# Padding tiles so that all operands of TensorE begin at one byte modulo 512, in a tuned encoder-layer kernel

## The chip, the cores and the metric

The kernel runs on one core of a Trainium2 chip, in one launch. The metric is the device time in microseconds (us), the median of several runs. A profile is one execution recorded by the hardware profiler. TensorE (PE) multiplies matrices; its loading of the stationary operand is listed apart, as PEld. VectorE (DVE), ScalarE (ACT) and GpSimd (POOL) do the element-wise work; SyncE (SP) issues most DMAs. On-chip memory has 128 partitions; a tile takes the same byte range in each of them, and "place" below means the first byte of that range.

## The reference

One layer on 1024 tokens of width 1024, in float32, with three sub-layers, each with an RMSNorm before and after and a residual sum:

```
h = rms_norm(x);  q, k, v, u, gates = split(h @ w_in)
o_attn = stick_breaking_attention(q, k, v)      # 8 heads x 64, strictly causal
o_ssm  = s5_branch(u)                           # complex-diagonal scan, gelu, sigmoid GLU
merged = gate_attn * (o_attn @ w_branch_attn) + gate_ssm * (o_ssm @ w_branch_ssm)
x = x + rms_norm(merged @ w_out)
x = x + rms_norm(cross_attention(rms_norm(x), mem))        # 4 heads, 256 memory tokens
x = x + rms_norm(conv_ffn(rms_norm(x)))         # up to 2 x 2816, causal conv 3, gelu gate, down
```

Stick-breaking attention weighs key s for query t by sigmoid(z_ts) times the product of (1 - sigmoid(z_tj)) over the keys j between them.

## The kernel before, in words

Every product is made in split precision: an operand is kept as a high part (rounded to the matmul's input format) and a low part (the rest), and `mm3` (L140 to L143) issues three matmuls for each 128-deep step: high x high, high x low, low x high. Nearly all of these are 128x128 weights against 512 moving columns. For each of them TensorE loads 128 columns of the stationary operand while the matmul before still runs.

The stages, in order of time:

- value and u projection (`tokens`, L423): hT, the normalised input (high and low, in pool ha), is stationary, in u with every eighth column; the weights move. The fourth chunk of these weights lies in two tiles of its own, wx (pool px).
- the S5 branch (`intra`, `flip_w`, `states`, `outputs`), its small matmuls and transposes set among jobs of the gate projection (`Job.step`, L265; hT moves), then the GLU (`glu_job`, L925): tiles yh, yl of pool pg move.
- stick-breaking attention (L996 to L1084): scores z from q, k, kl (pool pqk), sigmoids s1 and s2 (pool pat), a reversed scan on DVE, transposes of s1 with ident, then weighing (wth, wtl against vv). A list of groups with due times, made in advance, sets these among projection jobs: three 512-wide matmuls of a job, then one group.
- memory keys and values (`mem_k`, L1256, 256 wide; `mem_v`, L1270): the memory's tiles lie in pqk, reused as r_q and r_k; the merge of the branches (`merge`, L1316), whose moving operands lie in pqk (r_q, r_k, r_kl) and pc (oh, ol).
- output projection (`mix_out`, L1378), transposes of the new rows (xr in pool p5), queries, cross-attention (`xa_score` L1647, `xa_weigh` L1669, tiles pt, ph, pl in pool p6a) with projection steps between, its output projection, and the rows' norms (xr in pool p6).
- the gated MLP (`product`, L1905, then `mm_step`, L2186), by a seven-product scheme, from pools wpool, ha and hb; one early operand, S4a, lies in pool p6b.

In the first four stages and the output projection the order of instructions on TensorE, ScalarE, VectorE and GpSimd follows from due times (`at`, L227; `pe`, L797); later TensorE's order is the program's. SP takes DMAs in program order.

Pools are stacked: left pools from the bottom, right pools from the top of the memory. Within a pool, tiles lie in the order in which they are first asked for, rounded up to 32 bytes, the buffers of one tag side by side. When a pool is closed, the next one takes its place, and a tile's first write waits for the old tiles that it covers.

For attention's s1 rows there are four tags, one for each pair c of query blocks, each with two buffers that are (2c + 2) x 128 columns wide; block j = 0 of the pair uses (2c + 1) x 128 of them and j = 1 all.

By the declared sizes the tiles that TensorE reads begin at these bytes modulo 512:

| tiles | before | after |
|---|---|---|
| weights (wpool), hT and all of ha, all of hb | 288 | 288 |
| ident | 128 | 288 |
| wx (px); Tt, Ug, rc, y8 (pb) | 448 | 288 |
| U; W, F1, E1 (pt); yh, yl (pg) | 160 | 288 |
| Y1 | 480 | 288 |
| q, k, kl and r_q, r_k, r_kl (pqk); s1, vv, wth, wtl (pat); oh, ol (pc) | 480 | 288 |
| xr of p5 | 64 | 288 |
| pt; ph, pl (p6a) | 352; 416 | 288 |
| S4a (p6b) | 416 | 288 |
| xr of p6 | 32 | 32 |

Of the kernel before, what the change touches and what calls it, by code (L numbers as in the profile page):

```python
# [11 lines left out]
F32 = mybir.dt.float32  # L12
# [8 lines left out]
P = 128  # L21
# [24 lines left out]
def kernel(ctx: ExitStack, tc: tile.TileContext, a: dict, out: bass.AP, dbg=None):  # L46
# [4 lines left out]
    const = ctx.enter_context(tc.tile_pool(name="const", bufs=1, side="left"))  # L51
# [14 lines left out]
    td = [dpool.tile([4, P, 512], F32, name=f"td{q}") for q in range(NF // 2)]  # L66


    ident = const.tile([P, P], F32, name="ident")
    make_identity(nc, ident)  # L70
    zcol = const.tile([P, 1], F32, name="zcol")
    G.memset(zcol, 0.0)
    mhalf = const.tile([P, 1], F32, name="mhalf")
    G.memset(mhalf, -0.5)
    bgate = const.tile([P, 16], F32, name="bgate")
    bglu = const.tile([P, 4], F32, name="bglu")
    wr = ExitStack()
    pr_ = wr.enter_context(tc.tile_pool(name="pr", bufs=1, side="left"))
    gcol = pr_.tile([P, 2, KT], F32, name="gcol")
    rates_x = pr_.tile([P, 2, KT], F32, name="rates_x")  # L80
    rates_m = pr_.tile([P, 2], F32, name="rates_m")
    row_k = pr_.tile([P, 512], F32, name="row_k")
    rx_d = dpool.tile([KT, P], F32, name="rx_d")
    rm_d = dpool.tile([2, P], F32, name="rm_d")

# [38 lines left out]
    def f(ap):  # L124
        return ap.bitcast(F32)
# [87 lines left out]
    def gain_row(pool, name):  # L213
        g = pool.tile([P, D], F32, tag=name, name=name, bufs=1)
        dma(g, a[name].partition_broadcast(P))
        return g
# [10 lines left out]
    def at(t, go):  # L227
        heapq.heappush(events, (t, len(seen), go))
        seen.append(t)
# [48 lines left out]
    def rates_load(h):  # L278
        dma(row_k, rx_d[4 * h:4 * h + 4].rearrange("t p -> (t p)").partition_broadcast(P))
# [15 lines left out]
    def qk_job(pp, key):  # L295
        def out(t, h, sl, acc):
            Q, K, kl = qk[pp]
            hi, scale = (K, 1.0) if key else (Q, 0.125)

            lanes = [(slice(64 * i, 64 * i + 64), slice(64 - 64 * i, 128 - 64 * i)) for i in range(2)]  # L300

            def scaled(t):
                V.tensor_tensor(acc, acc, row_k, op=ALU.mult)
                rates_load(1 - h)

            def high(t):
                for i, (ln, xl) in enumerate(lanes):
                    C.mul(hi[i][ln, sl], acc[ln], scale)
                    if key:
                        dma(f(hi[i][xl, sl]), f(hi[i][ln, sl]))  # L310

            def low(t):
                for i, (ln, xl) in enumerate(lanes):
                    lo = kl[i][ln, sl] if key else hi[i][xl, sl]
                    V.scalar_tensor_tensor(lo, acc[ln], scale, f(hi[i][ln, sl]), op0=ALU.mult, op1=ALU.subtract)
                    if key:
                        dma(f(kl[i][xl, sl]), f(lo))

            if key:
                at(t, scaled)  # L320
            at(t + (0.8 if key else 0.0), high)
            at(t + (2.2 if key else 1.4), low)

        def start():

            qk[pp] = [[pqk.tile([P, S], F32R, tag=f"{n}{i}", name=f"{n}{i}") for i in range(2)] for n in ("q", "k", "kl")]

        return Job(a["w_in_T"][4 + pp if key else pp], out, start if key else None)

# [19 lines left out]
    pa = ra.enter_context(tc.tile_pool(name="pa", bufs=1, side="right"))  # L349
# [6 lines left out]
    U = pa.tile([P, 32, 8, 16], F32, name="U")  # L356
    sp = pq.tile([P, 3, 32], F32, name="sp")
    sbc = pq.tile([P, 4, 512], F32, name="sbc")
    dm = pa.tile([P, 32, 16], F32, name="dm")
    xt, rows_x, raw, pair = {}, {}, {}, {}  # L360
    sums_x = p0.tile([P, KT], F32, name="sums_x")

# [159 lines left out]
    turns = pa.tile([P, 7, 32], F32, name="turns")  # L522
    pr = pa.tile([P, 32, 9], F32, name="pr")
    pi = pa.tile([P, 32, 9], F32, name="pi")
    gc = [P, 32, 16]
    X, Xs, Y1, Y2 = (pa.tile(gc, F32, name=n) for n in ("X", "Xs", "Y1", "Y2"))

    def constants():
        G.memset(ec, math.e)
# [341 lines left out]
    while timed:  # L871
        t0, _, took, go, n = heapq.heappop(timed)
# [52 lines left out]
    def glu_job(m):  # L925
        def out(t, h, sl, acc):
            def put(t):
                if h == 0:
                    og[m] = open_g.pool.tile([P, S], F32, tag="og", name="og", bufs=2)
                C.activation(og[m][:, sl], acc, AF.Sigmoid, bias=bglu[:, m:m + 1])  # L930

            def gated(t):
                V.tensor_tensor(og[m][:, sl], og[m][:, sl], yT[m][:, sl], op=ALU.mult)
                if h:
                    dma(os_d[m], og[m])

            at(t, put)
            at(t + 0.8, gated)

        return Job(a["w_glu_T"][m], out, n=512, steps=4, operand=lambda k, sl: (yh[k][:, sl], yl[k][:, sl]))  # L940

    clock = max(clock, g0_ + 5.2)
    for m in range(4):
        j = glu_job(m)
# [18 lines left out]
    pqk = rqk.enter_context(tc.tile_pool(name="pqk", bufs=2, side="right", reuse_waits="tile"))  # L963
    rat = ExitStack()
    pat = rat.enter_context(tc.tile_pool(name="pat", bufs=2, side="right", reuse_waits="tile"))
# [28 lines left out]
    rows_of = {}  # L994

    def scores(t, n, c, j, n0, n1):  # L996

        (pp, hd), qi = divmod(n, 2), 2 * c + j
        Q, K, kl = qk[pp]
        nk = (qi + 1) * P  # L1000
        diag = n1 == nk
        qs = slice(qi * P, (qi + 1) * P)
        z = ps("z")[:, :n1 - n0]
        T.matmul(z, Q[hd][:, qs], K[hd][:, n0:n1], start=True, stop=False, skip_group_check=True)
        T.matmul(z, Q[hd][:, qs], kl[hd][:, n0:n1], start=False, stop=True, skip_group_check=True)  # L1005
        w = (n1 - n0) / 512.0

        def sig(t):
            if diag:
                rows_of[n, c, j] = (pat.tile([P, (2 * c + 2) * P], F32, tag=f"s1{c}", name="s1", bufs=2),  # L1010
                                    pat.tile([P, S], F32, tag="s2", name="s2", bufs=3))
            s1, s2 = rows_of[n, c, j]
            e = n1 - 1 if diag else n1
            if diag:
                G.memset(s1[:, e:n1], 0.0)
            C.activation(s2[:, n0:n1], z, AF.Sigmoid, scale=rates_x[:, 1, qi:qi + 1])  # L1016
            C.activation(s1[:, n0:e], z[:, :e - n0], AF.Sigmoid, scale=rates_x[:, 0, qi:qi + 1])

        def scan(t):
            s2 = rows_of[n, c, j][1]  # L1020
            add = begin[:, 512 - (n1 - n0):][:, ::-1] if diag else zcol.to_broadcast([P, n1 - n0])
            V.tensor_tensor_scan(s2[:, n0:n1][:, ::-1], s2[:, n0:n1][:, ::-1], add,  # L1022
                                 0.0 if diag else s2[:, n1:n1 + 1], op0=ALU.mult, op1=ALU.add)

        def rest(t):
            s1, s2 = rows_of[n, c, j]
            e = n1 - 1 if diag else n1
            G.tensor_tensor(s1[:, n0:e], s1[:, n0:e], s2[:, n0 + 1:e + 1], op=ALU.mult)  # L1028

        t += 0.5 * w + 0.4  # L1030
        at(t, sig)
        at(t + 0.7 * w + 0.2, scan)
        at(t + 2.2 * w + 0.5, rest)
# [76 lines left out]
    t, nf, begun, last_z = 0.0, 0, {}, 1e9  # L1110
# [110 lines left out]
    pool_of, row_of = {}, {}  # L1221
# [180 lines left out]

    def x1_load(t):
        x5[t] = pool_of["5"].tile([P, D], F32, tag="xr", name="xr", bufs=3)
        dma(x5[t], a["x"][t * P:(t + 1) * P, :])

    def x1_rates(h):
# [146 lines left out]
    p6 = r6.enter_context(tc.tile_pool(name="p6", bufs=1, side="right", reuse_waits="tile"))  # L1554
    gap = gain_row(p6, "g_xa_post")
    gfp = gain_row(p6, "g_ffn_pre")
    r6a = ExitStack()
    p6a = r6a.enter_context(tc.tile_pool(name="p6a", bufs=1, side="right", reuse_waits="tile"))

    have, yu, su, lows, again = {}, {}, {}, {}, [0]  # L1560

    def wo_chunk(x):
# [84 lines left out]
    def xa_score(h, hd, tp, fill):  # L1647

        qt = q2[h, hd // 2]
        sc = ps("a").rearrange("p (t m) -> p t m", t=2)  # L1650
        for t in range(2):
            ts_ = slice((2 * tp + t) * P, (2 * tp + t + 1) * P)
            for k in range(2):
                m = 2 * (hd % 2) + k
                mm3(sc[:, t], qt[:, 0, m, ts_], qt[:, 1, m, ts_], mk[:, 0, 2 * hd + k, :], mk[:, 1, 2 * hd + k, :],
                    k == 0, k == 1)
        fill(2)
        mx = p6a.tile([P, 2], F32, tag="mx", name="mx", bufs=2)
        V.reduce_max(mx, sc, axis=AX.X)
        V.tensor_scalar(mx, mx, -1.0 / 16, None, op0=ALU.mult)  # L1660
        pt = p6a.tile(s3, F32, tag="pt", name="pt", bufs=3)
        sm = p6a.tile([P, 2], F32, tag="sm", name="sm", bufs=2)
        for t in range(2):
            C.activation(pt[:, t], sc[:, t], AF.Exp, bias=mx[:, t:t + 1], scale=1.0 / 16, accum_out=sm[:, t:t + 1])
        V.reciprocal(sm, sm)
        V.tensor_tensor(pt, pt, bc(sm, 2, s3), op=ALU.mult)
        return pt
# [676 lines left out]
```

## Time and profile before

| | |
|---|---|
| median of 3 runs | 1656.94 us (1653.69 to 1658.94) |
| span of the profiled execution | 1653.9 us |
| instructions | 22415 |
| matmuls | 8062 |
| DVE, ACT, POOL busy | 1163.6, 880.1, 202.2 us |
| DMA | 279.26 MB, mean 169 GB/s |

How to read the lines below. A group's line has the source line, engine, operation, tiles as out<-in, shape and count; then busy time, mean ns of one and idle time of the engine before it, with what ended it. Matmuls are pipelined: the next starts before the one before it has ended, and the ends are modelled, so a duration of 0.39 us doesn't mean that matmuls start 0.39 us apart. The spacing of their starts is seen in the timeline (first column: start in us) or from a window's length and count. In a matmul's line one of the names after the arrow is the stationary and one the moving operand.

### The profile page before, as it was taken

Reading aid. Unit: us, or ns where it says so; the run is one execution under the profiler, and the core shown is the slowest. Engines: PE = TensorE matmul, PEld = TensorE weight load, DVE = VectorE, ACT = ScalarE, POOL = GpSimd, SP = SyncE. Lnnn points to the kernel's source line nnn. Section 1 sums busy time; section 2 is a strip of 40 time slices with the busy share of each in tenths; the row PEclk is TensorE's granted clock in tenths of the full one; section 3 lists DMA queues with packets and bytes.
Section 4 is the critical chain, followed back from the end, with each engine's and each line's share of the span. In section 5 each row is a group of like instructions: output and inputs, shape, how many; then the busy total and the mean of one; then the engine's idle time right before and its main releaser. Section 6 shows DMA issues by size and latency. Waiting matters only on the chain.

```text
span 1653.9 us, 22415 instructions
## 1 busy us (share of the span) xinstructions
PE 1633.8 (99%) x8062; PEld 1379.8 (83%) x8062; DVE 1163.6 (70%) x1616; ACT 880.1 (53%) x1459; POOL 202.2 (12%) x296
## 2 busy tenths in 40 slices
PE   9999999999999999999999999999999999999998
PEld 7998887888888988888888888888888888888886
DVE  6778637776866687467655678888887788775473
ACT  5434346676766544344444556656565556654441
POOL 5000002333332000011000000111111111000010
PEclk9999999999999999999999999999999999999999
DMA  9412144232433954464423574677777676688672
GB/s 323 124 46 66 61 144 110 71 102 80 113 99 127 336 190 136 158 211 158 141 69 129 205 271 175 187 210 211 214 195 206 186 203 185 210 311 280 192 237 81
DMA packets 125439, 279.26 MB, mean 169 GB/s; under 512 B 23696, under 2 KB 28304, under 8 KB 125200
## 3 DMA queue, kind: packets, MB, share of 16 engines
q1 hardware_dynamic: 113664, 251.35, 46.1%
q0 software_dynamic: 9360, 18.09, 6.3%
q10 hardware_dynamic: 2304, 8.39, 1.3%
q8 instruction: 63, 1.03, 0.3%
q14 instruction: 48, 0.39, 0.1%
HBM read 203.98 MB, written 67.38 MB: 164 GB/s over the span
## 4 chain that ended last, share of the span: by engine, by line
PE 89%; DVE 6%; DMA 2%; ACT 2%; issue 1%; POOL 0%; SPq 0%; DVEq 0%; POOLq 0%; ACTq 0%
PE ps_p L1921 8%; PE ps_p L1919 8%; PE ps_p L1920 8%; PE ps_f L141 7%; PE ps_f L143 7%; PE ps_f L142 6%; PE ps_d L2190 4%; PE ps_d L2189 4%; PE ps_d L2191 4%; PE ps_m L141 3%; PE ps_m L143 3%; PE ps_m L142 3%; PE ps_o L1067 2%; PE ps_w L1042 2%; PE ps_z L141 1%; PE ps_z L142 1%
## 5 line engine op out<-in xcount | busy, mean ns | idle before, releaser
L141 PE MATMUL ps_f<-hT,wh 128*128 128x512 f32 x384 | 161.3, 420 | 0.0
L143 PE MATMUL ps_f<-hT,wl 128*128 128x512 f32 x384 | 150.8, 393 | 0.0
L142 PE MATMUL ps_f<-hT,wh 128*128 128x512 f32 x384 | 150.6, 392 | 0.0
L1920 PE MATMUL ps_p<-qS,bm 128*128 128x512 f32 (+2 forms) x368 | 140.4, 382 | 1.7 <-DVE qS L1744 1.7
L1919 PE MATMUL ps_p<-qS,bm 128*128 128x512 f32 (+2 forms) x368 | 140.5, 382 | 1.4 <-DVE uu L1937 0.9
L1921 PE MATMUL ps_p<-qS,bm 128*128 128x512 f32 (+2 forms) x368 | 140.5, 382 | 0.0
L147 DVE TENSOR_TENSOR dn<-raw,dn 128x1024 fp32r<-128x1024 f32 x77 | 93.4, 1223 | 63.0 <-ACT dn L146 59.2
L146 ACT CAST dn<-raw 128x1024 fp32r<-128x1024 f32 x77 | 80.5, 1054 | 87.2 <-PE ps_d L2191 36.4
L2189 PE MATMUL ps_d<-dn 128*128 128x512 f32 x308 | 119.8, 389 | 0.0
L2190 PE MATMUL ps_d<-dn 128*128 128x512 f32 x308 | 119.8, 389 | 0.0
L2191 PE MATMUL ps_d<-dn 128*128 128x512 f32 x308 | 119.8, 389 | 0.0
L1028 POOL TENSOR_TENSOR s<-s,s 128x127 f32<-128x127 f32 (+4 forms) x96 | 89.9, 937 | 223.8 <-DVE s L1022 178.6
L1921 PE MATMUL ps_p<-qA,bm 128*128 128x512 f32 (+2 forms) x272 | 105.1, 386 | 0.5 <-DVE bm L1850 0.5
L1919 PE MATMUL ps_p<-qA,bm 128*128 128x512 f32 (+2 forms) x272 | 105.3, 387 | 0.0
L1920 PE MATMUL ps_p<-qA,bm 128*128 128x512 f32 (+2 forms) x272 | 105.0, 386 | 0.0
L1932 ACT COPY uu<-ps_p 128x512 f32<-128x512 f32 (+2 forms) x90 | 51.5, 572 | 90.0 <-PE ps_p L1921 90.0
L1862 POOL DMA_DIRECT2D bm<-in_ffn_up_T x61 | 52.7, 864 | 356.6 <-ACT bm L1861 144.2
L143 PEld LDWEIGHTS ps_f<-hT,wl 128*128 128x128 f32 x384 | 72.1, 188 | 16.3
L1016 ACT ACTIVATE s<-ps_z,rates_x 128x128 f32<-128x128 f32 (+3 forms) x96 | 56.3, 587 | 54.0 <-PE ps_z L1005 47.8
L1919 PEld LDWEIGHTS ps_p<-qS,bm 128*128 128x128 f32 x368 | 69.2, 188 | 15.2 <-ACT uu L1932 2.2
L1920 PEld LDWEIGHTS ps_p<-qS,bm 128*128 128x128 f32 x368 | 69.2, 188 | 15.1 <-DVE qS L1744 2.0
L1921 PEld LDWEIGHTS ps_p<-qS,bm 128*128 128x128 f32 x368 | 69.3, 188 | 13.2
(544 smaller groups left out, 4462.2 us busy)
## 6 DMA issues: line engine op xcount, KB each, us to landing
raw<-sd SPq DMA_DIRECT2D x77, 256.0 KB, 3.5
bm<-in_ffn_up_T POOLq DMA_DIRECT2D x61, 256.0 KB, 5.4
ws<-in_w_in_T SPq DMA_DIRECT2D x24, 512.0 KB, 3.3
ws<-in_xa_wo_N SPq DMA_DIRECT2D x23, 512.0 KB, 4.3
wv<-in_ffn_up_T SPq DMA_DIRECT2D x22, 512.0 KB, 4.0
wg<-in_ffn_up_T SPq DMA_DIRECT2D x22, 512.0 KB, 3.8
dr<-in_ffn_down SPq DMA_DIRECT2D x22, 512.0 KB, 6.4
td<-st SPq DMA_DIRECT2D x44, 256.0 KB, 5.9
```

The costliest lines, as they stand in the source:

```text
L141: T.matmul(acc, sh, mh, start=first, stop=False)
L142: T.matmul(acc, sh, ml, start=False, stop=False)
L143: T.matmul(acc, sl, mh, start=False, stop=last)
L146: C.copy(dh, src)
L147: (lo or V).tensor_tensor(dl, src, f(dh), op=ALU.subtract)
L1028: G.tensor_tensor(s1[:, n0:e], s1[:, n0:e], s2[:, n0 + 1:e + 1], op=ALU.mult)
L1919: T.matmul(acc, bm[:, 0, ks], q[:, 0, k, cs], start=alone and k == 0, stop=False, skip_group_check=True)
L1920: T.matmul(acc, bm[:, 0, ks], q[:, 1, k, cs], start=False, stop=False, skip_group_check=True)
L1921: T.matmul(acc, bm[:, 1, ks], q[:, 0, k, cs], start=False, stop=k == 3, skip_group_check=True)
L2189: T.matmul(acc[i], v[:, 0, 0, sl], v[:, 0, 1], start=first, stop=False, skip_group_check=True)
L2190: T.matmul(acc[i], v[:, 0, 0, sl], v[:, 1, 1], start=False, stop=False, skip_group_check=True)
L2191: T.matmul(acc[i], v[:, 1, 0, sl], v[:, 0, 1], start=False, stop=last, skip_group_check=True)
```

## The change

The tiles are moved; no instruction is added, removed or put elsewhere in its queue. In the constants' pool four small tiles (160 bytes in all) are asked for ahead of ident. In pool pr the row tile comes first, and a pad of 88 floats makes the small tiles after it come to 512 bytes. Pads of 48 floats in pqk, 96 in pa, 72 in p5, 32 in p6 and 96 in p6a shift what lies below them. In pa, five 2 KB tiles come right after U. In p6a, sm is asked for before pt. The s1 rows get one buffer for each block j, as wide as its row, in place of two of the wider width; that takes 2 KB less. A pad tile is never written or read.

```diff
+    zcol = const.tile([P, 1], F32, name="zcol")
+    mhalf = const.tile([P, 1], F32, name="mhalf")
+    bgate = const.tile([P, 16], F32, name="bgate")
+    bglu = const.tile([P, 4], F32, name="bglu")
     ident = const.tile([P, P], F32, name="ident")
     make_identity(nc, ident)
...
+    row_k = pr_.tile([P, 512], F32, name="row_k")
     gcol = pr_.tile([P, 2, KT], F32, name="gcol")
     rates_x = pr_.tile([P, 2, KT], F32, name="rates_x")
     rates_m = pr_.tile([P, 2], F32, name="rates_m")
-    row_k = pr_.tile([P, 512], F32, name="row_k")
+    pr_.tile([P, 88], F32, name="pad_r")
...
             qk[pp] = [[pqk.tile([P, S], F32R, tag=f"{n}{i}", name=f"{n}{i}") for i in range(2)] for n in ("q", "k", "kl")]
+            if pp == 0:
+                pqk.tile([P, 48], F32, name="pad_qk", bufs=1)
...
-    dm = pa.tile([P, 32, 16], F32, name="dm")
+    gc = [P, 32, 16]
+    X, Xs, Y1, Y2, dm = (pa.tile(gc, F32, name=n) for n in ("X", "Xs", "Y1", "Y2", "dm"))
...
-    gc = [P, 32, 16]
-    X, Xs, Y1, Y2 = (pa.tile(gc, F32, name=n) for n in ("X", "Xs", "Y1", "Y2"))
+    pa.tile([P, 96], F32, name="pad_a")
...
-                rows_of[n, c, j] = (pat.tile([P, (2 * c + 2) * P], F32, tag=f"s1{c}", name="s1", bufs=2),
+                rows_of[n, c, j] = (pat.tile([P, (2 * c + j + 1) * P], F32, tag=f"s1{c}{j}", name="s1", bufs=1),
                                     pat.tile([P, S], F32, tag="s2", name="s2", bufs=3))
...
         x5[t] = pool_of["5"].tile([P, D], F32, tag="xr", name="xr", bufs=3)
+        if t == 0:
+            pool_of["5"].tile([P, 72], F32, name="pad_5")
...
     gfp = gain_row(p6, "g_ffn_pre")
+    p6.tile([P, 32], F32, name="pad_6")
...
     p6a = r6a.enter_context(tc.tile_pool(name="p6a", bufs=1, side="right", reuse_waits="tile"))
+    p6a.tile([P, 96], F32, name="pad_6a")
...
         mx = p6a.tile([P, 2], F32, tag="mx", name="mx", bufs=2)
+        sm = p6a.tile([P, 2], F32, tag="sm", name="sm", bufs=2)
...
         pt = p6a.tile(s3, F32, tag="pt", name="pt", bufs=3)
-        sm = p6a.tile([P, 2], F32, tag="sm", name="sm", bufs=2)
```

More of the change, by code (lines that the diff above doesn't have):

```diff
@@ L66 @@
     td = [dpool.tile([4, P, 512], F32, name=f"td{q}") for q in range(NF // 2)]
+    zcol = const.tile([P, 1], F32, name="zcol")
+    mhalf = const.tile([P, 1], F32, name="mhalf")
+    bgate = const.tile([P, 16], F32, name="bgate")
+    bglu = const.tile([P, 4], F32, name="bglu")
     ident = const.tile([P, P], F32, name="ident")
     make_identity(nc, ident)
-    zcol = const.tile([P, 1], F32, name="zcol")
     G.memset(zcol, 0.0)
-    mhalf = const.tile([P, 1], F32, name="mhalf")
     G.memset(mhalf, -0.5)
-    bgate = const.tile([P, 16], F32, name="bgate")
-    bglu = const.tile([P, 4], F32, name="bglu")
     wr = ExitStack()
     pr_ = wr.enter_context(tc.tile_pool(name="pr", bufs=1, side="left"))
+    row_k = pr_.tile([P, 512], F32, name="row_k")
     gcol = pr_.tile([P, 2, KT], F32, name="gcol")
```

## The prediction

> **What bounds the kernel now.** I read the page first (busy time, slices, chain), then windows of single stages, then groups by form, then the timeline of TensorE where it changes from one kind of work to another.
>
> ```profile
> span 1653.9 us, 22415 instructions
> PE 1633.8 (99%) x8062; PEld 1379.8 (83%) x8062; DVE 1163.6 (70%) x1616; ACT 880.1 (53%) x1459; POOL 202.2 (12%) x296
> PE   9999999999999999999999999999999999999998
> PEclk9999999999999999999999999999999999999999
> PE 89%; DVE 6%; DMA 2%; ACT 2%; issue 1%; POOL 0%; SPq 0%; DVEq 0%; POOLq 0%; ACTq 0%
> ```
>
> TensorE is the bound from end to end: 99% busy, nine tenths or more in all slices but the last, at the full granted clock, and 89% of the chain. Nothing else can shorten the kernel by much; only a shorter time from one matmul's start to the next one's can. The change leaves the number and the order of the instructions as they are and moves tiles, so the question is whether a tile's place sets that time. The windows say by how much equal matmuls differ.
>
> ```profile
> core 0: us, PE busy (x) PEld busy (x) DVE busy (x) ACT busy (x) POOL busy (x), PEclk, DMA share, GB/s
> 218.50:240.50 22.00, 22.00 (x96) 17.72 (x95) 7.97 (x11) 9.18 (x13) 0.00 (x0) 1.00 0.44 157
> 260.00:535.00 275.00, 273.29 (x1525) 232.56 (x1524) 201.81 (x269) 193.15 (x403) 91.74 (x157) 1.00 0.34 97
> 583.00:671.00 88.00, 88.00 (x379) 70.91 (x378) 68.94 (x100) 41.33 (x59) 0.00 (x0) 1.00 0.46 147
> 1440.00:1640.00 200.00, 200.00 (x884) 165.64 (x884) 120.99 (x119) 92.17 (x108) 6.73 (x6) 1.00 0.67 227
> ```
>
> Columns: length, then busy time and count of each engine, granted clock, DMA. Three of these windows (GLU, branch merge, down projection) hold nothing but 128x512 matmuls without a gap. A matmul that only touches an edge is counted too, so the spacing is the length plus one duration (0.39 us) over the count: 88.39/379 = 233.2 ns in the merge, 22.39/96 = 233.2 ns in the GLU, 200.39/884 = 226.7 ns in the down projection. Clock, shape and number of weight loads are the same; DVE, ACT and DMA are busier in the fast window than in the GLU, so they aren't the cause. What differs is the place: in the down projection both operands begin at 288 modulo 512, in the merge the moving one at 480 and the weights at 288, in the GLU 160 and 288.
>
> The modelled duration in the groups by form carries the same 6 to 7 ns, which allows small groups to be compared:
>
> ```profile
> L2190 PE MATMUL ps_d<-dn 128*128 128x512 f32 x308 | 119.8, 389 | 0.0
> L141 PE MATMUL ps_z<-wh,mh 128*128 128x512 f32 x32 | 12.5, 390 | 0.0
> L142 PE MATMUL ps_w<-ol,wh 128*128 128x512 f32 x32 | 12.7, 396 | 0.0
> L142 PE MATMUL ps_f<-yl,wh 128*128 128x512 f32 x32 | 12.6, 395 | 0.0
> L142 PE MATMUL ps_z<-wl,r_q 128*128 128x512 f32 x8 | 3.2, 398 | 0.0
> L141 PE MATMUL ps_o<-wh,r_q 128*128 128x512 f32 x8 | 3.2, 396 | 0.0
> L142 PE MATMUL ps_m<-wx,hT 128*128 128x512 f32 x32 | 12.9, 402 | 0.0
> ```
>
> The first two rows have both operands at 288, the other five do not. The output projection right after the merge (ps_z<-wh,mh) is at 390, though it goes round the same four banks in the same way. So I take the place to be the cause there.
>
> **The change part by part.** Moving each tile to 288:
>
> (a) Branch merge, L1316: 8 x 2 x 2 x 4 x 3 = 384 matmuls in an unbroken run, 384 x (233.2 - 226.7) = -2.5 us. (b) GLU, L925: 4 x 2 x 4 x 3 = 96, 96 x 6.5 = -0.6 us. (c) Memory values, L1270: 96 matmuls at 397 (mean of the two r_q rows) against 389.5: -0.7 us. (d) wx in the value projection: 48 of the 96 wx matmuls have contiguous weights; their row mixes them with the u projection, so it gives bounds, from 0 to 48 x (402 - 389) = 0.6 us; I take half, -0.3 us, since the strided half can't become aligned. All four lie on the path, with hardly any idle time of TensorE in between: -4.1 us.
>
> [...]
>
> (e) Narrower matmuls. Here an aligned pair is not the faster one:
>
> ```profile
> L142 PE MATMUL ps_w<-r_k,wh 128*128 128x256 f32 x16 | 4.5, 281 | 0.0
> L143 PE MATMUL ps_a<-mk,q 128*128 128x256 f32 x64 | 18.1, 283 | 0.0
> L142 PE MATMUL ps_f<-hT,wh 128*128 128x512 f32 x384 | 150.6, 392 | 0.0
> L143 PE MATMUL ps_f<-hT,wl 128*128 128x512 f32 x384 | 150.8, 393 | 0.0
> L1004 PE MATMUL ps_z<-k,q 128*128 128x512 f32 x48 | 19.2, 400 | 0.0
> L1005 PE MATMUL ps_z<-kl,q 128*128 128x512 f32 x48 | 18.8, 393 | 0.0
> L142 PE MATMUL ps_m<-h2l,wh 128*128 128x512 f32 x88 | 34.4, 391 | 0.0
> ```
>
> The memory keys (r_k at 480, weights at 288) take 281, the cross-attention scores (both at 288) 283. Aligned, the 192 matmuls of L1256 should become like the scores: 192 x 2 = +0.4 us.
>
> (f) Mixed stages: SSM, stick-breaking attention (window 260 to 535, 1525 matmuls), cross-attention. hT and wh there are at 288 already, and still at 392 and 393, since every third matmul is followed by scores, transposes or weighting. Would aligning those others help? The timeline shows a stretch in which everything has been at 288 all along:
>
> ```profile
> start us, us, engine line op out<-in xcount [idle before <-releaser]
> 798.35 0.28 PE L142 MATMUL ps_a<-mk,q 128*128 128x256 f32 x1
> 798.47 0.28 PE L143 MATMUL ps_a<-mk,q 128*128 128x256 f32 x1
> 798.59 0.40 PE L141 MATMUL ps_m<-h2h,wh 128*128 128x512 f32 x1
> 798.82 0.40 PE L142 MATMUL ps_m<-h2l,wh 128*128 128x512 f32 x1
> 799.06 0.39 PE L143 MATMUL ps_m<-h2h,wl 128*128 128x512 f32 x1
> 799.29 0.40 PE L141 MATMUL ps_m<-h2h,wh 128*128 128x512 f32 x1
> 799.52 0.39 PE L142 MATMUL ps_m<-h2l,wh 128*128 128x512 f32 x1
> 799.75 0.39 PE L143 MATMUL ps_m<-h2h,wl 128*128 128x512 f32 x1
> 799.98 0.39 PE L141 MATMUL ps_m<-h2h,wh 128*128 128x512 f32 x1
> 800.20 0.39 PE L142 MATMUL ps_m<-h2l,wh 128*128 128x512 f32 x1
> ```
>
> After a row of 256-wide matmuls the first six 512-wide ones take 799.98 - 798.59 = 1.39 us, 232 ns each; only then do they settle. A change of width upsets the rhythm by itself, aligned or not, and it comes back after about six matmuls. Attention changes its work after three, so it never gets there. I take 0 for the mixed stages. Bounds: if all of their 512-wide matmuls fell to 389, 3 x 384 x 3.5 = 4.0 us (L141 taken like its two neighbours), 48 x (11 + 4) = 0.7 us for the z scores and 3 x 88 x 2.5 = 0.7 us for the queries, together -5.4 us. If they all took the 0.40 us of the passage above, the same 1,152 + 96 + 264 = 1,512 matmuls would cost 7 ns more each, +10.6 us. I stand near zero, since the passage (232 ns) and attention's rows (392 and 393, 3 to 4 above 389) agree.
>
> (g) Strided weights of the u projection (every eighth column of hT) and Tt's slices start at other bytes whatever the pool does: 0. FFN up and down: already at 288, and their pools don't move: 0.
>
> (h) Buffers and waits. The sigmoid rows: two buffers, used in turn by j = 0 and 1, become one of each j; each is rewritten one head later as before, so nobody waits longer. 4 x 512 bytes come free, which pay for the pads. No instruction is added (the pads are never written) and none changes its place in a queue. What can move is which old tile a new one lies on, and so what its first write waits for. The pools are shifted by 512 bytes or less (tiles inside attention's pool by up to 2 KB), so most tiles cover the same old ones. The one place that I found next to the path is g_xa_post's buffer in p6, which lay over 96 bytes of g_xa_pre's and now clears it:
>
> ```profile
> 789.50 1.28 DVE L1428 SCALAR_TENSOR_TENSOR xr<-y,rstd,g_xa_pre 128x1024 f32<-128x1024 f32 x1 [0.72 <-POOL rstd L210]
> 791.95 0.33 SPq L131 DMA_DIRECT2D ws<-in_xa_wq_T  x1
> 792.34 0.42 SPq L215 DMA_DIRECT2D g_xa_post<-in_g_xa_post  x1
> ```
>
> g_xa_pre was last read until 790.8, but on SP's queue the load stands behind a load of wq that goes at 791.95 anyway: 0. Had a shift gone the other way, that queue would hold up wq's later loads; I see none that does.
>
> Sum: -4.1 + 0.4 = -3.7 us. The profiled execution had a span of 1653.9 us and would come to 1650.2; that span is 3.0 us below the median of the runs, 1656.94, so a run comes to 1656.94 - 3.7 = 1653.2 us. A measurement of this kernel can tell about 0.3%, 5.0 us, from no change; the forecast is within it.
>
> **The rivals.** *All stages settle.* If it is the misaligned transposes, probabilities and values that upset the rhythm, attention settles too: -5.4 us on top, the +0.4 falls away: -4.1 - 5.4 = -9.5, 1647.4 us. For it: every break in attention today includes a tile at 480 or 128. Against it: the passage at 798, which is all aligned and upset. Chance 0.20.
>
> *The place is not the cause.* The slow runs share more than the byte: they read from the upper, right-hand pools. [...] Then nothing moves, 1656.9 us. Against it: the output projection takes moving weights and settles at once, and pools at 480, at 160 and at 448 are all slow. Chance 0.17.
>
> *Aligned reads collide (slower).* If a common start makes the weight load and the moving read meet at every line, long unbroken runs settle around it but broken ones pay each time. The 1,512 matmuls of (f) then take 0.40 us: +10.6 + 0.4 - 4.1 = +6.9, 1663.8 us. It undoes the gain from 3.7/1,512 = 2.4 ns per matmul on. For it: 281 against 283 in (e). Against it: the agreement in (f). Chance 0.06.
>
> **How the numbers follow.** My forecast has the rest, 0.57. Of it about 0.11 lies beyond 5.0 us of gain, where half of (f)'s lower bound comes true or the runs scatter (1653.69 to 1658.94 before); so faster by over 0.3%: 0.19 + 0.11 = 0.30; slower: 0.06; the same: 0.64. The range reaches half way into the first rival and takes in the second with scatter: 1648.2 to 1658.0. The forecast's own range is 1650 to 1656.
>
> **What would show it.** Right: in the merge, GLU and memory values the durations fall from 395-398 to 389-390 and the merge's windows give 227 ns; the memory keys rise from 281 to about 283; hT's rows in attention stay at 392 and 393; FFN as it was. Wrong: the merge still at 396 (second rival), hT at 389 (first), hT at 398 or more (third), or new idle time before TensorE at 792 to 810, which would mean that a moved tile made something wait.

## The result and the profile after

The changed kernel's median is 1652.3 us (21 runs, 1650.23 to 1656.01), the kernel before, beside it on the same chip, 1656.05 us (21 runs). The ratio is 0.9978 with a 95% interval of 0.9971 to 0.9985: 3.6 us less, 0.2%, with an interval of 2.5 to 4.8 us (the two medians themselves are 3.75 us apart). That is clear of zero and within the 0.3% that the prediction called no change. The forecast was 1653.2 us.

The page of the changed kernel has the same bound:

```profile
span 1651.9 us, 22414 instructions
PE 1632.3 (99%) x8062; PEld 1383.0 (84%) x8062; DVE 1163.5 (70%) x1616; ACT 880.3 (53%) x1459; POOL 202.2 (12%) x296
...
PEclk9999999999999999999999998999999999999999
...
PE 90%; DVE 5%; DMA 2%; ACT 2%; issue 1%; SPq 0%; POOL 0%; DVEq 0%; ACTq 0%; POOLq 0%
```

TensorE is still busy 99% of the time, with the same 8062 matmuls. One digit of the granted clock has gone from 9 to 8; it is taken up below. Now the windows of single stages (columns: length, then busy time and count of PE, PEld, DVE, ACT and POOL, granted clock, DMA). First the memory keys of the kernel before, which the prediction did not show as a window:

```profile
538.00:558.00 20.00, 20.00 (x172) 20.00 (x172) 13.85 (x17) 12.10 (x12) 0.10 (x1) 1.00 0.99 351
```

Then the changed kernel: attention, memory keys, merge and down projection.

```profile
260.00:535.00 275.00, 273.27 (x1525) 232.54 (x1525) 201.69 (x269) 193.17 (x402) 91.69 (x157) 1.00 0.33 98
538.00:558.00 20.00, 20.00 (x169) 20.00 (x168) 14.02 (x17) 11.33 (x12) 0.00 (x0) 1.00 0.98 345
583.00:671.00 88.00, 88.00 (x390) 72.75 (x389) 71.42 (x104) 42.81 (x61) 0.00 (x0) 1.00 0.49 157
1440.00:1640.00 200.00, 200.00 (x885) 165.58 (x884) 120.01 (x120) 90.88 (x107) 7.27 (x7) 1.00 0.68 226
```

Worked out as in the prediction (the length plus one duration, over the count), the merge went from 233.2 to 88.39/390 = 226.6 ns, the spacing of the down projection. The memory keys, 256 wide with a duration of 0.28 us, went the other way: 20.28/172 = 117.9 to 20.28/169 = 120.0 ns. Attention, whose odd tiles had all been moved, has the same 1525 matmuls in its 275 us.

The groups by form carry it line by line (mean ns of one is the number behind the comma; mm3's three lines are L142 to L144 in this kernel and L141 to L143 in the kernel before):

```profile
L142 PE MATMUL ps_f<-hT,wh 128*128 128x512 f32 x384 | 161.2, 420 | 0.0
L144 PE MATMUL ps_f<-hT,wl 128*128 128x512 f32 x384 | 150.8, 393 | 0.0
L143 PE MATMUL ps_f<-hT,wh 128*128 128x512 f32 x384 | 150.6, 392 | 0.0
L1007 PE MATMUL ps_z<-k,q 128*128 128x512 f32 x48 | 19.1, 399 | 0.0
...
L143 PE MATMUL ps_m<-wx,hT 128*128 128x512 f32 x32 | 12.8, 399 | 0.0
...
L143 PE MATMUL ps_w<-ol,wh 128*128 128x512 f32 x32 | 12.5, 390 | 0.0
L143 PE MATMUL ps_f<-yl,wh 128*128 128x512 f32 x32 | 12.4, 389 | 0.0
...
L143 PE MATMUL ps_w<-r_k,wh 128*128 128x256 f32 x16 | 4.5, 283 | 0.0
...
L143 PE MATMUL ps_z<-wl,r_q 128*128 128x512 f32 x8 | 3.1, 390 | 0.0
L142 PE MATMUL ps_o<-wh,r_q 128*128 128x512 f32 x8 | 3.1, 389 | 0.0
```

The merge (ol) is at 390 instead of 396, the GLU (yl) at 389 instead of 395, memory values (r_q) at 390 and 389 instead of 398 and 396, wx at 399 instead of 402, memory keys (r_k) at 283 instead of 281. hT's rows in attention and the z scores are where they were.

Summed over the starts of consecutive matmuls in the two traces:

| stage | spacing before, after (ns) | sum (us) |
|---|---|---|
| merge | 233.3, 226.8 | -2.51 |
| GLU | 233.3, 226.7 | -0.63 |
| memory values | 233.1, 227.2 (without two late starts in each) | -0.57 |
| wx with contiguous weights | 233.2, 226.9 | -0.3 |
| memory keys | 117.9, 120.2 | +0.43 |
| attention, whole stage | 512 wide: 242.1, 242.1 | -0.06 |
| all else | | +1.6 |

The first five come to -3.6 us, what the runs show. The profiled pair differs by only 2.0 us because of the last row, which isn't the place of tiles: mostly the passage where the MLP begins. Windows of TensorE alone over it (busy time and count, granted clock, DMA), before and then after:

```profile
1020.00:1040.00 20.00, 18.29 (x115) 0.91 0.30 85
```
```profile
1020.00:1040.00 20.00, 18.40 (x84) 0.74 0.32 92
```

In both traces TensorE runs at half clock for a part of this window (granted 0.50 from 1032 to 1034 before, from 1024 to 1034 after), in a stretch where it has waited for VectorE (1.52 us for qS, until 1028.63 before and 1024.51 after): a mean of 0.91 over 20 us is about 3.6 us at half clock, 0.74 about 10.4 us. In the profiled execution of the changed kernel the spell began earlier, at about 1023.8 against 1031.1 us (worked out from granted clocks of 0.94 in the window 1022 to 1024 and 0.77 in 1030 to 1032), and the passage took 2.85 us longer. Its length differs between single executions: in the profile of the first experiment below, this window has 0.91 again, in that of the kernel with ha and hb 256 bytes further on 0.83. Over the timed runs the mean granted clock lies between 0.995 and 0.999 for both kernels.

### The profile page after: what moved, and what is told of

It reads as the page before. It is cut to its first block, busy times and chain, and to the rows that moved or that the text cites. A ratio compares the mean times of both kernels' runs of the same rounds, so it can differ in the third digit from the quotient of the medians.

```text
span 1651.9 us, 22414 instructions
## 1 busy us (share of the span) xinstructions
PE 1632.3 (99%) x8062; PEld 1383.0 (84%) x8062; DVE 1163.5 (70%) x1616; ACT 880.3 (53%) x1459; POOL 202.2 (12%) x296
## 4 chain that ended last, share of the span: by engine, by line
PE 90%; DVE 5%; DMA 2%; ACT 2%; issue 1%; SPq 0%; POOL 0%; DVEq 0%; ACTq 0%; POOLq 0%
PE ps_p L1928 8%; PE ps_p L1927 8%; PE ps_p L1926 8%; PE ps_f L142 7%; PE ps_f L144 6%; PE ps_f L143 6%; PE ps_d L2198 4%; PE ps_d L2196 4%; PE ps_d L2197 4%; PE ps_m L143 3%; PE ps_m L142 3%; PE ps_m L144 3%; PE ps_o L1070 2%; PE ps_w L1045 2%; PE ps_z L142 1%; PE ps_z L144 1%
## 5 line engine op out<-in xcount | busy, mean ns | idle before, releaser
L142 PE MATMUL ps_f<-hT,wh 128*128 128x512 f32 x384 | 161.2, 420 | 0.0
L144 PE MATMUL ps_f<-hT,wl 128*128 128x512 f32 x384 | 150.8, 393 | 0.0
L143 PE MATMUL ps_f<-hT,wh 128*128 128x512 f32 x384 | 150.6, 392 | 0.0
L144 PEld LDWEIGHTS ps_f<-hT,wl 128*128 128x128 f32 x384 | 72.1, 188 | 16.1
```

Of the source, the lines that this page charges most:

```text
L142: T.matmul(acc, sh, mh, start=first, stop=False)
L143: T.matmul(acc, sh, ml, start=False, stop=False)
L144: T.matmul(acc, sl, mh, start=False, stop=last)
```

## The experiments

The theory to be tested: in long runs of 512-wide matmuls the spacing depends on the distance, modulo 512, between the first bytes of moving operand and weights, and only 0 is good. The rivals: the gain comes from something else in the change (the s1 rows' buffers, the order of the tiles); it depends on the absolute byte; or on a coarser or finer distance.

**Undo one part.** The pad in the pool of queries and keys is left out, so that pqk, pat and pc lie at 480 again and everything else is as in the changed kernel.

```diff
-            if pp == 0:
-                pqk.tile([P, 48], F32, name="pad_qk", bufs=1)
```

> The changed kernel without the pad in pqk: the tiles of pqk, pat and pc are back at 480 modulo 512, all others stay at 288. Theory (the distance between the places of moving and stationary operand sets the spacing): merge back at 233 ns from 227, memory values slower by 0.6 us in all, memory keys back at 118 ns from 120; the GLU stays at 227, attention as in both kernels. That gives back 2.5 + 0.6 - 0.4 = 2.7 us of the 3.6: a ratio to the kernel before of about 0.9994. Rival (the narrower s1 buffers or new covers of old tiles brought the time): the ratio stays at 0.998.

Measured: 1655.02 us, ratio 0.9992 (0.9983 to 1.0001). The merge's window:

```profile
583.00:671.00 88.00, 88.00 (x379) 70.93 (x378) 69.99 (x102) 40.58 (x59) 0.00 (x0) 1.00 0.46 146
```

It has 379 matmuls again, 233.2 ns. GLU and wx stay at 226.7 and 226.9 ns. So this one pad of 192 bytes is worth most of the gain, and the narrower s1 rows, which stay, bring nothing that shows. Attention takes as long as in the changed kernel (281.41 and 281.42 us), though its tiles lie at 480 here and at 288 there.

**Another byte for all.** Eight floats more ahead of ident, eight less in the pads behind, so that everything begins at 320.

```diff
+    const.tile([P, 8], F32, name="pad_0")
-                pqk.tile([P, 48], F32, name="pad_qk", bufs=1)
+                pqk.tile([P, 40], F32, name="pad_qk", bufs=1)
-    pa.tile([P, 96], F32, name="pad_a")
+    pa.tile([P, 88], F32, name="pad_a")
...
```

> The changed kernel with every place moved by 32 bytes: weights, activations and all pools at 320 modulo 512 instead of 288. Theory (distance): all spacings as in the changed kernel, 227 ns in merge and GLU, 120 for the memory keys, ratio 0.998. Rival (288 itself is the good place of an operand): merge, GLU and also the MLP, which nothing else touches, go to 230 ns or more, which would cost some 10 us in the MLP alone.

Measured: 1652.43 us, ratio 0.9977 (0.9968 to 0.9985). The merge:

```profile
583.00:671.00 88.00, 88.00 (x390) 72.84 (x390) 72.11 (x105) 41.73 (x60) 0.00 (x0) 1.00 0.47 155
```

390 matmuls, as in the changed kernel. At 320 for all it is as at 288 for all: the distance counts, not this byte.

**Which distances are good.** Two kernels with other pads (pad_a, pad_qk, pad_r and a new pad_c in pc) put stages at distances of their own.

```diff
-    pa.tile([P, 96], F32, name="pad_a")
+    pa.tile([P, 32], F32, name="pad_a")           # second kernel: 88
-                pqk.tile([P, 48], F32, name="pad_qk", bufs=1)
+                pqk.tile([P, 40], F32, name="pad_qk", bufs=1)   # second kernel: 112
+            if i == 3:
+                pool_of["c"].tile([P, 24], F32, name="pad_c", bufs=1)   # second kernel: 32
...
```

> Other distances, moving minus weights modulo 512, from the changed kernel: GLU 256, pqk 32, pc 448, wx 128. Theory with modulus 512: all of them slow, 231 to 238 ns in GLU and merge. Rival (the modulus is 256): the GLU at 227. [...] The memory keys, 256 wide, show whether a distance of 32 is like 0 (120 ns) or like 192 (118 ns).

> Other distances once more: GLU 32, pqk 256, pc 128, wx 64. Theory with modulus 512: GLU and both parts of the merge at 231 to 238 ns. Rival (modulus 256): the part of the merge that reads pqk at 227, the part that reads pc slow. [...]

Single runs: 1653.51 and 1653.74 us. The groups by form of the first, in which the GLU (yl) is at distance 256, the memory's tiles (r_q, r_k) at 32 and oh, ol at 448:

```profile
L143 PE MATMUL ps_w<-ol,wh 128*128 128x512 f32 x32 | 12.6, 394 | 0.0
L143 PE MATMUL ps_f<-yl,wh 128*128 128x512 f32 x32 | 12.4, 389 | 0.0
L143 PE MATMUL ps_w<-r_k,wh 128*128 128x256 f32 x16 | 4.5, 281 | 0.0
L143 PE MATMUL ps_z<-wl,r_q 128*128 128x512 f32 x8 | 3.2, 396 | 0.0
```

And of the second, with the GLU at 32, r_q and r_k at 256, oh and ol at 128:

```profile
L143 PE MATMUL ps_f<-yl,wh 128*128 128x512 f32 x32 | 12.6, 395 | 0.0
L143 PE MATMUL ps_w<-ol,wh 128*128 128x512 f32 x32 | 12.6, 394 | 0.0
L143 PE MATMUL ps_w<-r_k,wh 128*128 128x256 f32 x16 | 4.5, 283 | 0.0
L143 PE MATMUL ps_z<-wl,r_q 128*128 128x512 f32 x8 | 3.1, 390 | 0.0
```

Whatever is at 256 behaves as if it were at 0, both ways: 389 for the GLU, 390 for the memory values, and the slower 283 for the memory keys. From start to start:

| distance | stage, 512 wide | ns |
|---|---|---|
| 256 | GLU; memory values; merge, first part | 226.7; 227.2; 227.8 |
| 32 | GLU; merge, first part | 233.4; 232.7 |
| 64; 128 | wx | 232.5; 232.4 |
| 128; 448 | merge, second part | 232.6; 232.5 |
| 480 | memory values | 233.2 |

The modulus 512 fell: it is 256. Of the other multiples of 32 that were tried none is good, and they differ by 1 ns at most. In the first kernel, whose queries, keys and probabilities lie at distance 32, attention took 0.4 us longer than in the changed kernel (281.80 against 281.42 us).

**The same on a longer run.** A pad ahead of pool ha moves ha and hb, and with them the moving operand of FFN up, away from the weights: by 32 bytes in the first kernel, by 256 in the second (pad_r and pad_6a give the bytes back).

```diff
+    pha = ctx.enter_context(tc.tile_pool(name="pha", bufs=1, side="left"))
+    pha.tile([P, 8], F32, name="pad_ha")          # second kernel: 64
...
```

> The changed kernel with pools ha and hb moved by 32 bytes to 320, all else at 288: now the activations stand 32 bytes off the weights in the value projection, the output projection, the queries, the cross-attention's output and the whole up projection; the down projection has both operands in one tile and stays aligned. Theory: 6.4 ns each on 1742 matmuls of the up projection (11.1 us), 381 of the output projection (2.4), 286 of the cross-attention's output (1.7), 155 of the value projection, 118 query and some 350 gate and qk matmuls (3), down projection and attention unchanged: +18 us on the changed kernel, ratio to before about 1.009. Rival (only the pools that the change moved respond): ratio 0.998.

> As the kernel with ha and hb at 320, but moved by 256 bytes, to 32 modulo 512. Theory with modulus 256 (as the two runs with other distances showed in the GLU and the merge): nothing is lost, up projection at 226.7 ns, ratio 0.998. Rival (modulus 512): the same loss as at 32 bytes, ratio 1.009.

Measured: 1672.09 us at a distance of 32, ratio 1.0100 (1.0087 to 1.0113); 1651.89 us at 256, ratio 0.9977 (0.9968 to 0.9985). FFN up and the down projection at 32:

```profile
1050.00:1430.00 380.00, 378.71 (x1624) 304.08 (x1623) 302.06 (x388) 216.85 (x329) 49.19 (x57) 1.00 0.71 195
1440.00:1640.00 200.00, 200.00 (x882) 165.31 (x881) 126.64 (x120) 98.43 (x112) 5.66 (x4) 1.00 0.71 239
```

FFN up at 256:

```profile
1050.00:1430.00 380.00, 377.42 (x1666) 312.32 (x1665) 308.06 (x397) 219.37 (x335) 50.06 (x58) 1.00 0.73 204
```

At 32 FFN up has 1624 matmuls in 380 us, 1.29 us of them idle; at 256 it has 1666 in spite of 2.58 us of idle time. From start to start, without the waits, that is 233.4 and 226.7 ns. The down projection moved along with the pools, but has both operands in one tile, so its distance stays 0: 226.7 ns from start to start. It begins at 1453.8 us in this kernel, and the second window's first 14 us still belong to FFN up; hence its 882 matmuls. Attention, which the expectation had unchanged, took 1.0 us longer (282.46 against 281.42 us). So 32 bytes ahead of the wrong pool cost 1672.1 - 1652.3 = 20 us, more than five times what the whole change gains, about 12 of them in FFN up: the kernel before had its longest stage in the right place already.

**What the surcharge is.** In the spell at half clock 512-wide matmuls start 427 ns apart (rows in the last section). If nothing is on top there, which no run shows, the full clock would take 213 ns, and by this estimate even 226.7 has 13 ns on top, and 233.3 has 20. If the engine's reading of the next weights were in the way of the moving columns, fewer weights should cost less. Four kernels load 64 or 32 of the 128 weight columns in the merge; they leave out the other rows of its product, so their matmuls write fewer rows too, and the traces of single runs serve for the spacing alone. The first has the second part of the merge apart by 384, the next two have all tiles in their places, and the last has no pad_qk.

```diff
-        mm3(acc, *ch.part(slice(br * 512 + k * P, br * 512 + (k + 1) * P)), *o, k == 0, k == 3)
+        mm3(acc[:64], *ch.part(slice(br * 512 + k * P, br * 512 + k * P + 64)), *o, k == 0, k == 3)
...
```

> The changed kernel with half the weight columns in the branch merge: its matmuls load 64 of the 128 columns and write 64 rows, the other half of the merged rows is left out and set to zero; the tiles of pc stand at a distance of 384, so that half of the merge is aligned and half is not. At half clock 512 columns start every 427 ns, so a full-speed stream without any surcharge would be 213 ns, and the aligned spacing of 226.7 has 13 ns on top, the misaligned one of 233 has 20. Theory (the surcharge is the weight load's reads meeting the moving reads): half the columns, half the surcharge, 220 ns in the part that reads pqk and about 223 in the part that reads pc. Rival (a fixed cost of each matmul): 227 and 233 as before.

> The changed kernel, all tiles in their places, but the branch merge computes and loads only 64 of its 128 weight columns (the other 64 rows of the branch product are left out; 512 moving columns as before). [...] If a load of another length upsets the rhythm: 229 to 235 ns without settling, as in the run where half of the merge was apart.

> As the run before it, with 32 of the 128 weight columns (96 rows of the branch product are left out). [...] Fixed cost: 226.7 ns. Upset rhythm: about 230 ns.

> 64 of 128 weight columns in the merge (64 rows of the branch product are left out), and no pad in the pool of queries and keys, so that all moving tiles of the merge are apart from the weights (480 against 288), where full loads take 233.3 ns. [...]

In the first the part in its place takes 230.4 ns from start to start and the part apart 231.3, neither 220 nor 223, nor 227 and 233. The merge's window of the others, in this order:

```profile
583.00:671.00 88.00, 88.00 (x384) 52.11 (x383) 70.61 (x104) 41.37 (x60) 7.30 (x14) 1.00 0.47 149
```
```profile
583.00:671.00 88.00, 88.00 (x382) 42.17 (x380) 68.72 (x102) 39.41 (x57) 14.62 (x28) 1.00 0.47 148
```
```profile
583.00:671.00 88.00, 88.00 (x380) 51.73 (x379) 69.63 (x103) 40.26 (x60) 7.30 (x14) 1.00 0.46 145
```

The second pair of numbers after the length is the weight load: 72.75/389 = 187 ns with 128 columns (the changed kernel's row above), 136 with 64, 111 with 32. The spacing doesn't follow it: 226.6, 230.2, 231.4 ns in place, and 233.2, 232.6 apart. So the surcharge isn't paid per weight column. With half a load and all in place the starts go round in a fixed pattern (230, 236, 229, 224, 227, 234 ns) and never settle, although everything lies at one byte. Both the theory of the reads' number and that of a fixed cost of each matmul fell; an upset rhythm, which the expectations for the two kernels in place also name, is what the records show, without a cause for it (shorter load and fewer written rows come together here). What meets what inside TensorE stays open. Also not told apart: whether the moving operand's distance to its own weights counts or that to the weights loaded meanwhile, since in these runs both have the same place.

**A use of it that failed.** Since attention's 512-wide matmuls pay at each change of width (in hT's rows above 420 ns for the first of a step, 392 and 393 for the other two), fewer changes should help: its fill matmuls are issued in pairs of steps, six in a row before a group instead of three.

```diff
-        fill((22, 25, 28, 31)[g] if g < 4 else 38 + round((len(fills) - 38) * (g - 4) / (len(groups) - 4)))
+        fill((22, 25, 28, 31)[g] if g < 4 else 38 + 2 * round((len(fills) - 38) * (g - 4) / (len(groups) - 4) / 2))
```

> The changed kernel with attention's fill rounded to pairs: six 512-wide matmuls of a projection between two groups in place of three between one. Theory (a change of width upsets the rhythm whatever the places, and it comes back after some six matmuls): the stage from 257 to 537 us gets 1 to 2 us shorter, since the fourth to sixth matmul of a run stand at 228 to 231 ns and the first three at 232 to 235; ratio to before about 0.997. Rival (groups side by side wait for banks or for DVE): new idle time before TensorE in that stage, and it gets longer.

Measured: 1654.25 us, ratio 0.9991 (0.9983 to 1.0000), no better than the changed kernel. The groups of this kernel, to be held against those of the changed kernel above:

```profile
L142 PE MATMUL ps_f<-hT,wh 128*128 128x512 f32 x384 | 157.0, 409 | 0.0
...
L1070 PE MATMUL ps_o<-wth,vv 128*128 128x256 f32 x128 | 35.5, 293 | 0.0
...
L1007 PE MATMUL ps_z<-k,q 128*128 128x512 f32 x48 | 20.3, 422 | 0.0
...
L1007 PE MATMUL ps_z<-k,q 128*128 128x384 f32 x16 | 6.0, 378 | 0.0
```

The two of the changed kernel that were not shown:

```profile
L1070 PE MATMUL ps_o<-wth,vv 128*128 128x256 f32 x128 | 33.9, 281 | 0.0
...
L1007 PE MATMUL ps_z<-k,q 128*128 128x384 f32 x16 | 5.4, 340 | 0.0
```

The first matmul of each step fell from 420 to 409 as hoped (-4.2 us). But now two groups follow each other, and the first matmul of a group pays instead: z scores 399 to 422 (512 wide) and 340 to 378 (384 wide), weighing 281 to 293, together +3.4 us. From start to start attention's 512-wide matmuls gave 3.7 us, its narrower ones and transposes took back 3.0, and waits of TensorE grew by 1.2 us; in all the stage took 0.6 us longer. A change between kinds of work has its price between two groups too; pairing moves it.

## Why the prediction was right

The forecast of -3.7 us met -3.6, and its main steps came as described. That the two agree to 0.1 us is luck: the runs' interval is 2.5 to 4.8 us, (d) was half of a bound, and a delay that (h) did not have takes back about 0.3 us. The forecast time is 0.9 us off because its base was: a median of 3 runs, 1656.94 us, where 21 runs gave 1656.05.

- (a) merge, -2.5: measured -2.51. (b) GLU, -0.6: -0.63. (c) memory values, -0.7: -0.57; their mean is 227.2 ns, not 226.7, since the first six after the 256-wide keys take 231 ns each. (d) wx, -0.3: -0.3, the value at half way between bounds.
- (e) memory keys, +0.4: +0.43. In these 256-wide matmuls the tiles in one place are the slower ones; the modelled rows 281 and 283 told the sign and the size.
- (f) mixed stages, 0: attention -0.06 us, hT's rows unmoved. The rival that all stages settle needed them at 389; its argument, that each break includes a misaligned tile, is answered by the runs with attention at 480 and at 288, which are equal. Their place is not wholly without effect: at distance 32 attention lost 0.4 and 1.0 us in the two kernels above. The passage that the prediction used against it looks the same in the changed kernel:

```profile
798.82 0.28 PE L144 MATMUL ps_a<-mk,q 128*128 128x256 f32 x1
798.93 0.40 PE L142 MATMUL ps_m<-h2h,wh 128*128 128x512 f32 x1
...
800.32 0.39 PE L142 MATMUL ps_m<-h2h,wh 128*128 128x512 f32 x1
```

Six matmuls in 1.39 us again, 232 ns each. The rival of colliding reads needed hT's rows to rise; they are at 420, 392 and 393 before and after, and it fell with them.
- The rival that the place is not the cause fell with the merge's spacing alone, and the run that took one pad back shows it from the other side: 233.2 against 226.6 ns. FFN up has 233.4 against 226.7 ns in the kernels with ha and hb 32 and 256 bytes further on, with nothing changed but the distance. What the cause is inside TensorE, no run here shows.
- (h) waits, 0: not quite. No new wait came at 792 to 810. But at 54 us a matmul of the value projection starts late in the changed kernel, after a low part of the weights (L393):

```profile
53.37 0.41 PE L142 MATMUL ps_m<-wh,hT 128*128 128x512 f32 x1
54.38 0.64 PE L143 MATMUL ps_m<-wl,hT 128*128 128x512 f32 x1 [0.60 <-DVE wl L393]
54.86 0.40 PE L144 MATMUL ps_m<-wh,hT 128*128 128x512 f32 x1
```

With the usual 0.24 us between starts, 1.0 us is lost here. The same place costs 0.6 us in the first experiment and 0.1 to 0.4 us, mostly 0.3, in the seven other kernels whose value projection has all operands in place. In the four where wx or the whole projection is apart (the kernel before, the two with other distances, ha and hb at 32) the delay is missing. So it is the faster projection that overtakes VectorE's conversion, and about what (d) gains is lost again. In six of the experiments the memory values have a wait of 0.04 to 0.76 us for a low part of the weights at 577 to 578 us, which the kernels before and after don't have. It doesn't go with the place, and its cause is open.

What the prediction had wrong without harm: it called the distance one modulo 512. Of the places before the change none was at a distance of 256, so no term hung on it. Its argument that the pools at 480, 160 and 448 are all slow was right for a reason that it didn't have, and half of the freedom in choosing pads went unseen.

## What to carry to other kernels

In long unbroken runs of 512-wide matmuls with a new 128-column load each, let moving operand and weights begin at the same byte modulo 256; in this kernel it is worth 6.6 ns of 233 (3%) per matmul, and a pad of a few bytes anywhere in a stack of pools can lose it for a stage that the edit doesn't touch (20 us here). Count the matmuls in a window of each long stage and compare the spacings before looking for anything else. Don't expect it in stages that change their shape every few matmuls (attention here: 1 us of 281 at most), nor in 256-wide ones, where the same place costs 2 ns. A faster stage can run into a wait that it did not have, as the value projection did.

## What the runs showed of the hardware that was not expected

- The distance counts modulo 256 bytes; 32, 64, 128, 160, 192 and 224 modulo 256 all cost about 6 to 7 ns (starts 232.4 to 233.4 ns apart, against 226.7 at 0 and, in the GLU, at 256).
- In the merge, 512-wide matmuls in one place that load 64 or 32 weight columns, and write as many rows, start 230.2 and 231.4 ns apart, against 226.6 with 128.
- At half clock the distance made no difference: 427 ns from start to start at 0 and at 32. In the changed kernel's timeline (start, modelled duration), where the granted clock is 0.50 (window 1030 to 1032):

```profile
1030.44 0.63 PE L1928 MATMUL ps_p<-qA,bm 128*128 128x512 f32 x1
1030.86 0.63 PE L1926 MATMUL ps_p<-qA,bm 128*128 128x512 f32 x1
1031.29 0.63 PE L1927 MATMUL ps_p<-qA,bm 128*128 128x512 f32 x1
```

And in the kernel with ha and hb at 32, where the moving operand of these matmuls is apart from the weights, at the same clock (window 1036 to 1040):

```profile
1036.46 0.63 PE L1930 MATMUL ps_p<-qA,bm 128*128 128x512 f32 x1
1036.89 0.63 PE L1928 MATMUL ps_p<-qA,bm 128*128 128x512 f32 x1
1037.31 0.63 PE L1929 MATMUL ps_p<-qA,bm 128*128 128x512 f32 x1
```

Starts are 0.85 us for two in both, 427 ns apart over the whole spell; at the full clock matmuls of this kind are 226.7 and 233.4 ns apart in the two kernels. That is 13 and 20 ns more than half of 427. What these go to, no run here shows.
